# Second products of experts and MLP: activations held in the array, 512 weight features passing

## The chip, the cores and the metric

The kernel runs on one core of one Trainium2 chip. The metric is the device time of one execution in microseconds; the kernel before took 3621.57 us (median of three runs, 3618.63 to 3621.67). TensorE multiplies, VectorE (DVE), ScalarE (ACT) and GpSimd (POOL) do the elementwise work, and SyncE (SP) issues the loads.

## The reference, cut to what matters

256 tokens of 2048 features pass through two blocks. The first ends with a layer of 16,384 experts, of which each token takes 128 with gates; the second ends with an MLP of 8192 hidden features. What the change touches are the last lines of the two:

```python
    # experts (block 1): rows of exp_v, summed with the weights of the chosen experts
    a = jax.nn.gelu(jnp.einsum('cd,chkd->chk', xc, u))
    w = gc * a
    out = jnp.einsum('chk,chkd->cd', w, exp_v[ec])
    ...
    # MLP (block 2)
    x = x + jnp.square(jax.nn.relu(h2 @ w_up[l])) @ w_down[l]
return rmsnorm_2(x, g_final)
```

## The kernel before, in words

All activations lie with features on the 128 partitions and the 256 tokens in the columns. Nothing is gathered: every expert is multiplied for every token, and the gate of an expert that was not chosen is zero. So the experts are two dense products with 16,384 hidden features, in 16 groups of 1024 (8 tiles of 128), and the MLP is the same with 8 groups of 1024.

Every product runs in three parts. `load_half` (L163) loads 128 x 1024 fp32 weights into `raw` (4 buffers), ScalarE rounds them into `wh` (L168), and VectorE takes the rest into `wl` (L169); `wh` and `wl` have 3 buffers each. Activations are a `Pair` of a rounded part and a rest. `mm3` (L186) then gives high times high (L187), high times rest (L188) and rest times high (L189). The first operand of `T.matmul` stands in the array (its load is the LDWEIGHTS, in the profile PEld), the second passes.

The second product of a group is `down` (L1233). It runs over 16 tiles of 128 output features; `gemm_tile` (L206) sums 8 hidden tiles into 256 columns of a bank `mm`, 24 matmuls of 128 weight features in the array and 256 tokens passing. So a group has 16 x 24 = 384 matmuls and takes 16 halves of weights. After each tile a function is called. For the experts it is `moe_done` (L1276): group 0 copies the bank into `total` on ScalarE, groups 1 to 14 add it there on VectorE (L1282), group 15 adds it, times `g2`, to the stream `xs` (L1286), sums the squares of the stream for two norms (`ss3`, `ss4`: a Square on ScalarE (L273) into one of two buffers `sqt`, then an addition (L274), on POOL for the first 14 tiles), and makes the first operand `hp` of block 2 (L286, L287). For the MLP it is `mlp_done` (L1541), which adds each bank to the stream (L1543) and in the last group sums its squares.

A scheduler sets the order of each engine's instructions from the order in which the program is written and its own costs; each engine then takes them strictly in that order. `total` uses two buffers `act`. After group 15 come the two sums over partitions (L224), the turned norms (L253) and, among them, the first products of block 2 (`w_in2`, from L1373 on). Banks: `mm` has 3, `aux` 3 and `acc` 2 buffers of [128, 512] fp32.

Of the kernel before, what the change touches and what calls it, by code (L numbers as in the profile page):

```python
# [17 lines left out]
L = 256  # L18
# [9 lines left out]
# groups of experts whose first products go ahead  # L28
AHEAD = 7
# blocks of 512 modulation values that TensorE takes, and tiles of 128 that VectorE takes  # L30
PE_ADA = [4, 5, 6, 7, 0, 1, 2, 3, 8, 9, 10, 11]
DVE_ADA = list(range(48, 96))
# buffers of raw weights, of their parts, of the modulation's tiles, and of gates that wait for branches
NRAW, NW, NADR, NGT = 4, 3, 2, 18
# the gates of 4 tokens: microseconds of VectorE, and how many steps their rows go ahead of their products
GATE_COST, LEAD = 1.8, 2
# tiles of the modulation for VectorE after each weight tile of a phase of block 1
SLOW = ([1] * 9, [0] * 4, [0] * 6 + [1] * 2, [2] * 4, [1] * 16)
# microseconds of VectorE for the work that waits, after each weight tile
PEER_PUMP, MIX_PUMP = (2.6, 2.6, 3.5), (1.8, 1.8, 2.0, 1.8)  # L40

# columns of the packed per-channel vectors
# [12 lines left out]
# columns of the constants, which depend on shapes alone  # L55
# [8 lines left out]
# those that stay, those of the state space operators, those of the attention  # L64
# [10 lines left out]
def body(top, tc, nc, V, S, G, T, I, out):  # L75
# [28 lines left out]
    # ---------------------------------------------------------------- constants  # L104
# [19 lines left out]
    # work that fills in between weight tiles: (cost on VectorE in us, function)  # L124
# [24 lines left out]
    # ------------------------------------------------- weights: load and split  # L149
# [5 lines left out]
    def load_behind(dst, src):  # L155
        """A load that waits for its turn behind the weights before it."""
        if last_load[0] is None:
            nc.sync.dma_start(dst, src)
        else:
            with tc.issue_after(ins_of(last_load[0])):  # L160
                nc.sync.dma_start(dst, src)
# [13 lines left out]
    # where the modulation's tiles go, and how many  # L175
# [15 lines left out]
    class Pair:  # L191
        """Activations as float32r high and low parts, 8 feature tiles to a buffer."""
# [8 lines left out]
    def split(dst, src, eng=None):  # L201
        """dst = (high, low) of the fp32 src."""
        S.activation(dst[0], src, AF.Copy)
        V.tensor_tensor(dst[1], src, dst[0].bitcast(F32), op=OP.subtract)
# [8 lines left out]
    # ------------------------------------------------------------------- norms  # L213
    def row_sum(acc):
        """Sum of acc over partitions, on every partition."""
# [4 lines left out]
    def token_sum(acc):  # L220
        """Sum of acc over partitions, by tokens on partitions [128, 2]."""
# [8 lines left out]
    def rsqrt_tok(m):  # L230
        """1/sqrt(m); a Newton step after the engine's square root."""
# [9 lines left out]
    def rstd_tok(p, n):  # L241
        """1/sqrt(p/n + eps) of sums by tokens."""
# [4 lines left out]
    def spread_tok(y, turned=False):  # L247
        """A value by token, from [128, 2] to every partition [128, L]; turned: from tokens (j, c) to (c, j)."""
# [28 lines left out]
    def scaled_pair(dst, src, gain, rstd, shift, scp):  # L277
        """dst pair = src * gain * rstd + shift."""
# [5 lines left out]
    def gained(dst, src, gain):  # L284
        """dst pair = src * gain."""
# [3 lines left out]
    # ================================================================== block 1  # L289
# [9 lines left out]
    # silu(c), by partitions in column 0 of a block of 32 for TensorE, and on every partition for VectorE  # L299
# [11 lines left out]
    def early_raw():  # L311
        """Before the products start, buffers of later uses take the tiles too: one or two pieces."""
# [7 lines left out]
    def ada_parts(b, early=False):  # L320
        """512 modulation values: four column groups of the array take four row tiles at a time."""
# [42 lines left out]
    # the norm of the input  # L364
# [5 lines left out]
    # products of the state space inputs run block by block of features: two tiles in a bank, opened with zeros  # L370
# [5 lines left out]
    # columns: sh1, sc1, g1, sh2, sc2, g2  # L376
# [4 lines left out]
    def u_block(b):  # L381
        """What 512 features give to the state space inputs."""
# [23 lines left out]
    # ---- SSM parameters, on [(parity, state), pair of groups]  # L406
# [91 lines left out]
    def cmul(ore, oim, are, aim, bre, bim, t1, t2, minus=None, eng=V):  # L498
        """o = a * b; with minus = -are, the imaginary part with its sign turned."""
# [7 lines left out]
    def ssm_params():  # L507
        dt = expo(ld)
        # exp and sin, cos of the exponent of a and of its multiples that the tables start from
# [11 lines left out]
        # powers a^0 .. a^4 and the input weights a^(3-j) * w  # L521
# [29 lines left out]
        # phasor tables: e^(i 4 theta b) and e^(i 32 theta a)  # L551
# [17 lines left out]
        # the input weights, by [j, part, pair] rows, to DRAM  # L569
# [16 lines left out]
    def ssm_pre(t):  # L586
        """The operators of four pairs of groups: of the inputs, of the states, and within a chunk."""
# [43 lines left out]
    # ---------------------------------------------------------------- SSM tiles  # L631
# [6 lines left out]
    def ssm_store_u(t, p):  # L638
        """Channels (parity, h, pair) and tokens 4c + j, to rows (parity, j, h) and columns (pair, c)."""
# [8 lines left out]
    def ssm_in(t):  # L648
# [4 lines left out]
        # taps by distance, then by input and output place in the chunk  # L653
# [15 lines left out]
        # chunk inputs, turned back by the phase at the chunk  # L669
# [74 lines left out]
    # feature tiles 0-1 k_cmp, 2-3 v_cmp, 4 gates, 5-6 k_slc, 7-8 k_win, 9-16 q, 17-20 v  # L744
# [33 lines left out]
    # ------------------------------------------------------- compressed keys  # L778
# [7 lines left out]
    def compress(s):  # L786
        """Keys (s = 0) by features, values (s = 1) by key rows: four column groups of the array, 32 blocks in each."""
# [47 lines left out]
    # gates to token rows  # L835
# [440 lines left out]
    def moe_done(d, p):  # L1276
        xt, sm = xs[d // 8][:, d % 8], total[d // 8][:, d % 8]
        if g == 0:
            S.activation(sm, p, AF.Copy)  # L1279
            return  # L1280
# [425 lines left out]
```

## Time and profile before

| what | value |
|---|---|
| median of three runs | 3621.57 us |
| profiled execution, span | 3613.3 us |
| matmuls of the second products of the experts | 3 x 2048 |
| matmuls of the second products of the MLP | 3 x 1024 |
| last expert group ends | 2193 us |
| last matmul of the MLP starts | 3596.02 us |

The profiled execution's own time is not listed apart from its span; the median stands 8.3 us over the span. In the page, a matmul's mean time includes the time that it needs from its first column to its end, and neighbours overlap in it: the pace of a stretch is read from the distance of starts or from the count in a stretch, not from the mean.

### The profile page before, as it was taken

Reading aid. Unit: us, or ns where it says so; the run is one execution under the profiler, and the core shown is the slowest. Engines: PE = TensorE matmul, PEld = TensorE weight load, DVE = VectorE, ACT = ScalarE, POOL = GpSimd, SP = SyncE. Lnnn points to the kernel's source line nnn. Section 1 sums busy time; section 2 is a strip of 40 time slices with the busy share of each in tenths; the row PEclk is TensorE's granted clock in tenths of the full one; section 3 lists DMA queues with packets and bytes.
Section 4 is the critical chain, followed back from the end, with each engine's and each line's share of the span. In section 5 each row is a group of like instructions: output and inputs, shape, how many; then the busy total and the mean of one; then the engine's idle time right before and its main releaser. Section 6 shows DMA issues by size and latency. Waiting matters only on the chain.

```text
span 3613.3 us, 71254 instructions
## 1 busy us (share of the span) xinstructions
PE 3525.4 (98%) x29284; PEld 3421.0 (95%) x29284; DVE 2485.9 (69%) x4064; ACT 1667.9 (46%) x2438; POOL 355.2 (10%) x318
## 2 busy tenths in 40 slices
PE   6899988999999999999999999999999999999998
PEld 3678888999999999999999999999999999999998
DVE  6485888899967555555555679887655666666665
ACT  2234844469954444444444445345444443343444
POOL 3442041016600000000000012000000000000000
PEclk8899999999999999999999999999999999999999
DMA  8888685556677666666656655555555555555554
GB/s 312 313 293 287 237 312 176 176 180 223 234 247 239 220 217 218 220 216 219 196 193 208 218 183 179 186 176 180 184 184 182 181 182 185 182 184 184 182 184 143
DMA packets 227749, 759.76 MB, mean 210 GB/s; under 512 B 26888, under 2 KB 64144, under 8 KB 211936
## 3 DMA queue, kind: packets, MB, share of 16 engines
q1 hardware_dynamic: 219440, 747.27, 61.1%
q0 software_dynamic: 1648, 5.57, 0.5%
q8 instruction: 230, 3.77, 0.4%
q10 hardware_dynamic: 6336, 2.36, 0.2%
q14 instruction: 95, 0.78, 0.1%
HBM read 731.91 MB, written 23.21 MB: 209 GB/s over the span
## 4 chain that ended last, share of the span: by engine, by line
PE 88%; DVE 6%; DMA 2%; issue 1%; ACT 1%; POOL 1%; ACTq 0%; SPq 0%; DVEq 0%; POOLq 0%
PE mm L189 27%; PE mm L187 27%; PE mm L188 27%; DVE wl L169 2%; PE acc L333 1%; DVE gst L1206 1%; POOL t L1030 1%; DVE oh L1187 1%; ACT wh L168 1%; DVE oh L1186 0%; DVE va L1361 0%; PE u L403 0%; PE aux L340 0%; PE aux L658 0%; DMA udr<-t 0%
## 5 line engine op out<-in xcount | busy, mean ns | idle before, releaser
L168 ACT ACTIVATE wh<-raw 128x1024 fp32r<-128x1024 f32 x1126 | 1190.0, 1059 | 1654.1 <-PE mm L188 1465.4
L169 DVE TENSOR_TENSOR wl<-raw,wh 128x1024 fp32r<-128x1024 f32 x1126 | 1382.9, 1231 | 640.3 <-ACT wh L168 628.7
L189 PE MATMUL mm<-hp,wl 128*128 128x256 f32 x5168 | 1470.6, 285 | 4.9 <-DVE wl L169 4.9
L187 PE MATMUL mm<-hp,wh 128*128 128x256 f32 x5168 | 1470.0, 285 | 4.3 <-ACT hp L281 2.5
L188 PE MATMUL mm<-hp,wh 128*128 128x256 f32 x5168 | 1467.0, 284 | 0.8 <-DVE hp L282 0.8
L187 PEld LDWEIGHTS mm<-hp,wh 128*128 128x128 f32 x5168 | 993.9, 193 | 12.0 <-issue 5.2
L189 PEld LDWEIGHTS mm<-hp,wl 128*128 128x128 f32 x5168 | 994.2, 192 | 10.6 <-DVE wl L169 7.3
L188 PEld LDWEIGHTS mm<-hp,wh 128*128 128x128 f32 x5168 | 994.4, 193 | 5.7 <-issue 4.1
L187 PE MATMUL mm<-p,wh 128*128 128x256 f32 x2048 | 579.9, 283 | 0.9 <-ACT act L1279 0.9
L188 PE MATMUL mm<-p,wh 128*128 128x256 f32 x2048 | 579.7, 283 | 0.0
L189 PE MATMUL mm<-p,wl 128*128 128x256 f32 x2048 | 579.5, 283 | 0.0
L187 PEld LDWEIGHTS mm<-p,wh 128*128 128x128 f32 x2048 | 393.5, 192 | 1.1 <-ACT act L1279 1.1
L188 PEld LDWEIGHTS mm<-p,wh 128*128 128x128 f32 x2048 | 393.5, 192 | 0.0
L189 PEld LDWEIGHTS mm<-p,wl 128*128 128x128 f32 x2048 | 393.2, 192 | 0.2 <-DVE wl L169 0.2
L187 PE MATMUL mm<-hid,wh 128*128 128x256 f32 x1024 | 289.8, 283 | 0.0
L188 PE MATMUL mm<-hid,wh 128*128 128x256 f32 x1024 | 289.8, 283 | 0.0
L189 PE MATMUL mm<-hid,wl 128*128 128x256 f32 x1024 | 289.8, 283 | 0.0
L187 PEld LDWEIGHTS mm<-hid,wh 128*128 128x128 f32 x1024 | 196.6, 192 | 0.0
L188 PEld LDWEIGHTS mm<-hid,wh 128*128 128x128 f32 x1024 | 196.6, 192 | 0.0
L189 PEld LDWEIGHTS mm<-hid,wl 128*128 128x128 f32 x1024 | 196.6, 192 | 0.0
L1282 DVE TENSOR_TENSOR act<-mm,act 128x256 f32<-128x256 f32 x224 | 95.0, 424 | 123.1 <-PE mm L189 123.1
L1190 POOL TENSOR_TENSOR row<-oh,gl 128x512 fp32r<-128x512 f32 x64 | 137.1, 2158 | 304.1 <-DVE gl L1264 222.7
(448 smaller groups left out, 3549.3 us busy)
## 6 DMA issues: line engine op xcount, KB each, us to landing
raw<-in_peer_u SPq DMA_DIRECT2D x256, 512.0 KB, 4.2
raw<-in_peer_v SPq DMA_DIRECT2D x256, 512.0 KB, 4.2
raw<-in_w_up SPq DMA_DIRECT2D x128, 512.0 KB, 3.6
raw<-in_w_down SPq DMA_DIRECT2D x128, 512.0 KB, 3.7
raw<-in_w_in SPq DMA_DIRECT2D x110, 512.0 KB, 4.4
adr<-in_w_ada_dve SPq DMA_DIRECT2D x48, 1024.0 KB, 6.6
raw<-in_w_gate SPq DMA_DIRECT2D x96, 512.0 KB, 3.5
adr<-in_w_ada_pe SPq DMA_DIRECT2D x32, 1024.0 KB, 5.6
```

What stands on the lines that cost most here:

```text
L168: S.activation(wh, r, AF.Copy)
L169: last_split[0] = ins_of(V.tensor_tensor(wl, r, wh.bitcast(F32), op=OP.subtract))
L187: T.matmul(p, w[0], x[0], start=st, stop=False)
L188: T.matmul(p, w[0], x[1], start=False, stop=False)
L189: T.matmul(p, w[1], x[0], start=False, stop=sp)
L333: T.matmul(p[32 * j:32 * j + 32], csel[:, 4 * c + j], raws[j // n][:, 512 * (j % n):512 * (j % n) + 512], start=(c == 0), stop=(c == 3), t ...
L1030: G.tensor_tensor(t1, t1, t2, op=OP.add)
L1187: V.tensor_tensor(oh2, io, fan(eslot[:, 1]), op=OP.is_equal)
L1190: G.tensor_tensor(row[:, :, 1], oh1, fan(gl), op=OP.mult)
L1206: V.tensor_tensor(o, p[:, :, 1], o, op=OP.add)
L1282: V.tensor_tensor(sm, p, sm, op=OP.add)
```

## The change

`down` is turned round. What stands in the array is now a 128-token half of an activation part, and 512 weight features pass. For each of 4 blocks `c` of 512 output features it takes two banks (one for each half of the tokens, `acc` for even and `aux` for odd blocks) and sums all 8 hidden tiles into them: 4 halves of weights, each with 2 hidden tiles and 12 matmuls of 512 columns. A group so has 4 x 48 = 192 matmuls instead of 384, and as many columns pass in all. The sums lie by token rows: `total` and, for the MLP, a new `summed` are added to from the two banks, 512 columns at a time (in the changed file L1251 for the first group, L1253 for the others). Only in the last group of each (`d_done` given) the four feature tiles of a block are turned back by 8 transposes (L1260) into `mm` banks and the old function is called on them. The stream is added to once, and not in each MLP group. The weights' layout on the host changes to match (`_tm`).

```diff
-    def down(src, w, d_done):
-        for dp in range(8):
-            hv = load_w(src[dp])
-            for f in range(2):
-                p = gemm_tile(hv, list(range(8 * f, 8 * f + 8)), w)
-                d_done(2 * dp + f, p)
+    def down(src, w, total, first, d_done=None):
+        for c in range(4):
+            ps = [aux_bank() if c % 2 else acc_bank() for _ in range(2)]
+            for q in range(4):
+                wh, wl = load_half(src[c, q])
+                for e in range(2):
+                    xh, xl = w[2 * q + e]
+                    cols = slice(512 * e, 512 * e + 512)
+                    for i, p in enumerate(ps):
+                        t = slice(128 * i, 128 * i + 128)
+                        T.matmul(p, xh[:, t], wh[:, cols], start=(q + e == 0), stop=False)
+                        T.matmul(p, xl[:, t], wh[:, cols], start=False, stop=False)
+                    for i, p in enumerate(ps):
+                        T.matmul(p, xh[:, 128 * i:128 * i + 128], wl[:, cols], start=False, stop=(q == 3 and e == 1))
+            for i, p in enumerate(ps):
+                o = total[i].rearrange("p a t -> p (a t)")[:, 512 * c:512 * c + 512]
+                if first:
+                    S.activation(o, p, AF.Copy)
+                else:
+                    V.tensor_tensor(o, p, o, op=OP.add)
+            if d_done is None:
+                continue
+            for d in range(4 * c, 4 * c + 4):
+                p = mm_bank()[:, :L]
+                for i in range(2):
+                    T.transpose(p[:, 128 * i:128 * i + 128],
+                                total[i].rearrange("p a t -> p (a t)")[:, 128 * d:128 * d + 128], ident)
+                d_done(d, p)
...
     def moe_done(d, p):
-        xt, sm = xs[d // 8][:, d % 8], total[d // 8][:, d % 8]
-        if g == 0:
-            S.activation(sm, p, AF.Copy)
-            return
-        if g < NG - 1:
-            V.tensor_tensor(sm, p, sm, op=OP.add)
...
+        xt = xs[d // 8][:, d % 8]
         V.scalar_tensor_tensor(xt, p, g2[:, d:d + 1], xt, op0=OP.mult, op1=OP.add)
...
-        down(I["peer_v"][g], w, moe_done)
+        down(I["peer_v"][g], w, total, g == 0, moe_done if g == NG - 1 else None)
...
+    summed = [tl(ml, [128, 8, L], F32, "sum", 2) for _ in range(2)]
...
-        down(I["w_down"][g], hid.pop(g), mlp_done)
+        down(I["w_down"][g], hid.pop(g), summed, g == 0, mlp_done if g == 7 else None)
```

Three places show how the instructions move. The first is TensorE inside the last expert group (`p` are the weighted activations, rounded part and rest); before:

```order
L187 MATMUL mm_25855<-p_3719_25235,wh_25817 128x256
L188 MATMUL mm_25855<-p_3720_25236,wh_25817 128x256
L189 MATMUL mm_25855<-p_3719_25235,wl_25818 128x256
L187 MATMUL mm_25855<-p_3719_25235,wh_25817 128x256
L188 MATMUL mm_25855<-p_3720_25236,wh_25817 128x256
L189 MATMUL mm_25855<-p_3719_25235,wl_25818 128x256
```

and after:

```order
L1244 MATMUL acc_22117<-wh_22121,p_3599_22099 128x512
L1245 MATMUL acc_22117<-wh_22121,p_3600_22100 128x512
L1244 MATMUL acc_22118<-wh_22121,p_3599_22099 128x512
L1245 MATMUL acc_22118<-wh_22121,p_3600_22100 128x512
L1247 MATMUL acc_22117<-wl_22122,p_3599_22099 128x512
L1247 MATMUL acc_22118<-wl_22122,p_3599_22099 128x512
```

Two hidden tiles gave six matmuls of 256 columns for one tile of 128 features; one hidden tile now gives six of 512 columns for four such tiles.

The second place is TensorE where the last expert group ends and block 2 begins (`hp` is the operand of block 2, `mm_25958` its first sum). Before:

```order
L188 MATMUL mm_25855<-p_3720_25236,wh_25817 128x256
L189 MATMUL mm_25855<-p_3719_25235,wl_25818 128x256
L187 MATMUL mm_25958<-hp_25249,wh_25948 128x256
L188 MATMUL mm_25958<-hp_25251,wh_25948 128x256
L189 MATMUL mm_25958<-hp_25249,wl_25949 128x256
```

After (`mm_22678` is that sum):

```order
L1247 MATMUL aux_22485<-wl_22544,p_3599_22099 128x512
L1247 MATMUL aux_22486<-wl_22544,p_3599_22099 128x512
L1260 MATMUL mm_22561<-con_71,act_1170_6339 128x128
L1260 MATMUL mm_22573<-con_71,act_1170_6339 128x128
L1260 MATMUL mm_22585<-con_71,act_1170_6339 128x128
L1260 MATMUL mm_22561<-con_71,act_1171_6340 128x128
L1260 MATMUL mm_22573<-con_71,act_1171_6340 128x128
L1260 MATMUL mm_22585<-con_71,act_1171_6340 128x128
L1260 MATMUL mm_22597<-con_71,act_1170_6339 128x128
L1260 MATMUL mm_22597<-con_71,act_1171_6340 128x128
L187 MATMUL mm_22678<-hp_22113,wh_22668 128x256
```

The eight transposes of the last block stand directly behind its last matmul and ahead of block 2. Those of each of the three blocks before stand in three pieces inside the next block, the first behind its first 3 or 4 matmuls, the last behind 9 or 10.

The third place is ScalarE in the last expert group, where it rounds weights (L168) between the work for the feature tiles (L273 Squares, L286 operand of block 2). Before:

```order
L286 ACTIVATE hp_25249<-b_950_5035,gmix_12531 128x256
L168 ACTIVATE wh_25491<-raw_25489 128x1024
L273 ACTIVATE sqt_25401<-b_950_5035 128x256
L273 ACTIVATE sqt_25404<-b_950_5035,vec_73 128x256
L286 ACTIVATE hp_25249<-b_950_5035,gmix_12531 128x256
L168 ACTIVATE wh_25497<-raw_25495 128x1024
```

After (`wh_22295` is the last quarter of the second block):

```order
L273 ACTIVATE sqt_22217<-b_950_5035 128x256
L273 ACTIVATE sqt_22220<-b_950_5035,vec_73 128x256
L286 ACTIVATE hp_22113<-b_950_5035,gmix_12531 128x256
L273 ACTIVATE sqt_22229<-b_950_5035 128x256
L273 ACTIVATE sqt_22232<-b_950_5035,vec_73 128x256
L286 ACTIVATE hp_22113<-b_950_5035,gmix_12531 128x256
L168 ACTIVATE wh_22295<-raw_22293 128x1024
L168 ACTIVATE wh_22365<-raw_22363 128x1024
L168 ACTIVATE wh_22383<-raw_22381 128x1024
```

One tile's three instructions alternated with one rounding of weights; now the twelve of four tiles stand in a row, and the roundings behind them in a row.

## Rows read from the trace of the kernel before

**Rows 1.** Page, part 1: busy us (share of the span) xinstructions.

```profile
PE 3525.4 (98%) x29284; PEld 3421.0 (95%) x29284; DVE 2485.9 (69%) x4064; ACT 1667.9 (46%) x2438; POOL 355.2 (10%) x318
```

**Rows 2.** Waits of TensorE, 1040 to 3600 us, the longest: us, times, longest us.

```profile
PE aux L224 <- DVE ssq L274: 1.4, 1, 1.4
```

**Rows 3.** Page, part 5, second products: xcount | busy us, mean ns | idle before.

```profile
L187 PE MATMUL mm<-p,wh 128*128 128x256 f32 x2048 | 579.9, 283 | 0.9 <-ACT act L1279 0.9
...
L187 PE MATMUL mm<-hid,wh 128*128 128x256 f32 x1024 | 289.8, 283 | 0.0
```

**Rows 4.** Stretches: PE, PEld, DVE, ACT, POOL busy (instructions), PEclk, DMA, GB/s.

```profile
1037.00:1039.90 2.90, 2.90 (x16) 2.90 (x15) 2.89 (x5) 1.45 (x2) 0.00 (x0) 0.50 0.92 302
1200.00:1400.00 200.00, 200.00 (x1669) 200.00 (x1668) 115.85 (x125) 82.66 (x97) 0.00 (x0) 1.00 0.66 222
...
3200.00:3400.00 200.00, 200.00 (x1669) 200.00 (x1668) 121.00 (x157) 79.69 (x88) 0.00 (x0) 1.00 0.56 184
```

**Rows 5.** Timeline of TensorE in the experts: start us, us, engine line.

```profile
2000.05 0.28 PE L187 MATMUL mm<-p,wh 128*128 128x256 f32 x1
2000.17 0.28 PE L188 MATMUL mm<-p,wh 128*128 128x256 f32 x1
```

**Rows 6.** Timeline of the weight loads at the same place.

```profile
2000.05 0.19 PEld L188 LDWEIGHTS mm<-p,wh 128*128 128x128 f32 x1
```

**Rows 7.** Timeline of TensorE in the stretch of granted clock 0.50.

```profile
1038.36 0.41 PE L187 MATMUL mm<-hp,wh 128*128 128x256 f32 x1
1038.58 0.41 PE L188 MATMUL mm<-hp,wh 128*128 128x256 f32 x1
```

**Rows 8.** Timeline of TensorE, two starts twelve matmuls apart, behind a wait.

```profile
516.72 0.28 PE L189 MATMUL mm<-qy,wl 128*128 128x256 f32 x1
...
518.11 0.28 PE L189 MATMUL mm<-hp,wl 128*128 128x256 f32 x1
```

**Rows 9.** Timeline of TensorE, three merged runs: one-column products, slower products, transposes.

```profile
232.74 1.02 PE L340 MATMUL aux<-ones,adaz 128*128 128x1 f32 x8
...
370.30 1.03 PE L818 MATMUL aux<-con,cz 128*128 128x256 f32 x4
...
410.61 0.82 PE L943 MATMUL aux<-con,lg 128*128 128x128 f32 x6
```

**Rows 10.** Groups of ScalarE and VectorE; the last: ns shortest, median, longest.

```profile
L168 ACT ACTIVATE wh<-raw 128x1024 fp32r<-128x1024 f32 x882 | 933.6, 1059 | 1413.0 <-PE mm L188 1292.1 <-issue 89.3 <-DVE co L1402 9.1
...
L169 DVE TENSOR_TENSOR wl<-raw,wh 128x1024 fp32r<-128x1024 f32 x883 | 1079.7, 1225 | 543.7 <-ACT wh L168 532.3
...
L1226 DVE TENSOR_TENSOR act<-act,p x40: 682/686/695, 1029.7 to 2066.6; 128x512 f32<-128x512 f32 x40
```

**Rows 11.** Timeline of POOL, VectorE and ScalarE for the squares and the stream.

```profile
558.68 0.74 POOL L274 TENSOR_TENSOR ssq<-ssq,sqt 128x256 f32<-128x256 f32 x1 [1.11 <-ACT sqt L273]
...
2157.14 2.35 POOL L274 TENSOR_TENSOR ssq<-ssq,sqt 128x256 f32<-128x256 f32 x2 [0.53 <-ACT sqt L273]
...
2158.82 0.47 DVE L1286 SCALAR_TENSOR_TENSOR b<-mm,g,b 128x256 f32<-128x256 f32 x1
...
2160.20 0.49 ACT L286 ACTIVATE hp<-b,gmix 128x256 fp32r<-128x256 f32 x1
```

**Rows 12.** Timeline of TensorE where the experts end.

```profile
2192.89 0.28 PE L189 MATMUL mm<-p,wl 128*128 128x256 f32 x1
2193.01 0.28 PE L187 MATMUL mm<-hp,wh 128*128 128x256 f32 x1
...
2200.86 0.64 PE L253 MATMUL aux<-diag,ones 128*128 128x256 f32 x2
```

**Rows 13.** Timeline where the MLP ends.

```profile
3596.02 0.28 PE L189 MATMUL mm<-hid,wl 128*128 128x256 f32 x1
...
3597.25 0.42 DVE L274 TENSOR_TENSOR ssq<-ssq,sqt 128x256 f32<-128x256 f32 x1 [0.48 <-ACT sqt L273]
```

More of the change, by code (lines that the diff above doesn't have):

```diff
@@ L1276, in moe_done @@
     def moe_done(d, p):
-        xt, sm = xs[d // 8][:, d % 8], total[d // 8][:, d % 8]
-        if g == 0:
-            S.activation(sm, p, AF.Copy)
-            return
-        if g < NG - 1:
-            V.tensor_tensor(sm, p, sm, op=OP.add)
-            if g == NG - 2:
-                V.scalar_tensor_tensor(xt, sm, g2[:, d:d + 1], xt, op0=OP.mult, op1=OP.add)
-            return
+        xt = xs[d // 8][:, d % 8]
         V.scalar_tensor_tensor(xt, p, g2[:, d:d + 1], xt, op0=OP.mult, op1=OP.add)
@@ L1539, in body, with mlp_done @@
             mlp_up(g + 1)
-        def mlp_done(d, p, last=(g == 7)):
+        def mlp_done(d, p):
             xt = xs[d // 8][:, d % 8]
             V.tensor_tensor(xt, p, xt, op=OP.add)
-            if last:
-                ss6.add(xt)
-                S.activation(xt, xt, AF.Copy, scale=VC("g_final")[:, d:d + 1])
-        down(I["w_down"][g], hid.pop(g), mlp_done)
+            ss6.add(xt)
+            S.activation(xt, xt, AF.Copy, scale=VC("g_final")[:, d:d + 1])
+        down(I["w_down"][g], hid.pop(g), summed, g == 0, mlp_done if g == 7 else None)
     r6 = rstd_of(ss6.acc, D)
@@ L1562, in _fm, with _tm @@
     return np.ascontiguousarray(w.reshape(k // 128, 128, f // 128, 128).transpose(2, 1, 0, 3)).reshape(f // 128, 128, k)
+def _tm(w):
+    return w.reshape(-1, 4, 2, 128, 4, 512).transpose(0, 4, 1, 3, 2, 5).reshape(-1, 4, 4, 128, 1024)
 def _cols(v):
@@ L1621, in layout @@
     r["peer_u"] = a["peer_u"][0].reshape(128, 128, 16, 128).transpose(0, 3, 2, 1).reshape(128, 128, D)
-    r["peer_v"] = a["peer_v"][0].reshape(128 // GE, GE, 128, 8, 2, 128).transpose(0, 3, 2, 4, 1, 5).reshape(128 // GE, 8, 128, D)
+    r["peer_v"] = _tm(a["peer_v"][0])
     w = a["w_in_2"][0].reshape(D, 34, 128)
@@ L1632, in layout @@
     r["w_up"] = _fm(a["w_up_2"][0])
-    r["w_down"] = a["w_down_2"][0].reshape(8, 8, 128, 8, 2, 128).transpose(0, 3, 2, 4, 1, 5).reshape(8, 8, 128, D)
+    r["w_down"] = _tm(a["w_down_2"][0])
     dsk = a["ssm_d"][0].reshape(32, 2, 16).transpose(1, 2, 0)
```

## The prediction

> **What bounds the kernel now.** I read the page first: TensorE is busy 98% of the span [rows 1]. Busy time of overlapping matmuls is no pace, so I went on to the waits. From 1040 us to the end of the MLP TensorE has five waits in the list, the longest 1.4 us in total [rows 2]. So in that part the time is matmuls times pace, and a count divided into a stretch gives the pace: 1669 matmuls in 200 us of experts, and again 1669 in 200 us of MLP, are 119.8 ns each at granted clock 1.00, which is the 2.4 GHz level [rows 4]. The timeline shows the same, starts 0.12 us apart [rows 5]. The mean of 283 ns [rows 3] is no pace, since neighbours overlap.
>
> 256 columns at 2.4 GHz, one a cycle, would be 106.7 ns. What are the other 13 ns? Three views help. In a stretch at granted clock 0.50 (1.2 GHz) starts are 0.21 to 0.22 us apart [rows 7], and 256 / 1.2 = 213.3: where the columns pass slowly, nothing is added. Eight matmuls of a single column, each with its own load of 128 columns, take 1.02 us, the last 0.27 of it its own length: (1.02 - 0.27) / 7 = 107 ns, so loads alone have a pace near that of 256 columns [rows 9]. And each load starts together with the matmul before its own [rows 5, 6]. My reading: the next load takes up to 120 ns from there, and a matmul whose columns pass in 107 ns waits for it. With 512 columns (213.3 ns) the load is over long before.
>
> The four products at L818 pass 256 columns slowly at the full clock: (1.03 - 0.38) / 3 = 217 ns [rows 9], about 213.3 and 2 to 4 more. So I take 215.7 ns for the new matmul: 213.3 and the 2.4 ns between that row's reading (up to 217) and the bare stream. Bounds: 213.3 (nothing added) and 240 (120 ns per 256 columns, whatever the cause).
>
> The Trainium skill, "TensorE: Matmul & The Clock Gate", section "Back-to-back issue gap", gives the isolated gap as 262 cycles for 256 columns and 518 for 512, that is 109 and 216 ns. The second is my value; the first is contradicted by 119.8 ns here. By the page alone the change would save 9216 x 109 - 4608 x 216 = 9 us, less than it costs; the measurement decides for the old matmul, and no run here shows the new one.
>
> **The change part by part.**
>
> *Matmuls.* Removed: 3 x 2048 and 3 x 1024 [rows 3], 9216 x 120 ns = 1105.9 us. Added: 24 groups x 192 = 4608 x 215.7 = 993.9 us. Gain 112.0 us; by the bounds 123 (at 213.3) and 0 (at 240).
>
> *Weights.* A half of weights serves 12 matmuls, 2.59 us instead of 24 x 0.12 = 2.88. Rounding and rest take 1.06 + 1.23 = 2.29 us one after the other, on two engines [rows 10], so neither is over half busy with it, and three buffers put two halves (5.2 us) between a split and its use. DMA must bring 512 KB in 2.59 us, 202 GB/s; 302 stand in the rows at one place, 222 in the experts [rows 4]. Taken as nothing; without that cover it is the rival below.
>
> *Sums.* 16 additions of 256 columns become 8 of 512, 0.69 us each by the addition of that size [rows 10], while TensorE works on the other pair of banks for 10.4 us. Nothing on the path.
>
> *Transposes.* 64. Six in a row take 0.82 us, so (0.82 - 0.27) / 5 = 0.11 each [rows 9]: 7.0 us of TensorE, 3.5 in each last group. The Trainium skill, same page, section "Part 4: PE-mode transpose", puts one at about 275 ns inside a kernel; by that it would be 17.6 us and the time some 10 us more. The run of six decides for 0.11.
>
> *Last expert group.* Here I expect the largest loss. The feature tiles now come four at once, every 10.4 us. Each needs two Squares on ScalarE, which write two buffers that POOL empties by additions. POOL takes 2.35 us for two additions beside VectorE's work and 0.74 for one alone [rows 11]. With VectorE less busy in the burst I take 0.93 each, nearer to the lone one. ScalarE takes its twelve instructions for four tiles in order, and the rounding of the block's last quarter of weights stands behind them. From the end of the block before: two sums (2 x 0.62), a transpose (0.3) and the stream's update (0.47 [rows 11]) bring the first Square to 2.4 us; its addition starts at 2.8. The eighth Square waits for the sixth addition, 2.8 + 6 x 0.93 = 8.4; Square and operand, 0.4 + 0.49 [rows 11], end at 9.3, then 1.06 + 1.23 of splitting: 11.6. TensorE wants that quarter after three quarters and the transposes, 3 x 2.59 + 0.9 = 8.7. So a block waits some 3 us; the first has two additions fewer and waits 1.4. In the third that rounding is ahead of the burst, but then block 2's first weights are behind it, and the last sums stand behind those on VectorE. Following the four queues row by row with these durations, blocks two to four take 2.9, 4.0 and 1.4 us over 10.35 (transposes in it), 6.9 us pass between the last matmul and block 2's first, where it was 0.12 [rows 12], and 1.6 us more are lost to the norms' sums (before, the norm's product came 7.85 us behind block 2's first matmul [rows 12]). Together 16.8. With additions of 0.74 it is 13, with 1.18 it is 22. Take 17.
>
> *Last MLP group.* Here VectorE adds the squares, and no POOL. Mid-group transposes 24 x 0.11 = 2.6 us and three short waits for the sums, 0.3 each. At the end, the square's addition of the last tile ended 3597.67 - 3596.02 = 1.65 us behind the last matmul's start [rows 13]; now two sums (to 1.5), transposes (to 1.8) and four tiles with updates, Squares and scalings in turn on ScalarE, 0.9 each, end at about 5.3. Plus 3.7; nothing hides it, as everything behind it is serial. Together 7, bounds 5 and 11. Saved additions to the stream in groups 1 to 7 were hidden and give nothing.
>
> Sum: 112 - 17 - 7 = 88 us off 3613.3, 3525.3; with the 8.3 us that the median stands over that span, **3533.6 us**. Its own range: pace 213.3 to 218 (gain 123 to 101), costs 18 to 33, and up to 10 more of short waits: 3517 to 3564.
>
> **The rivals.**
>
> *The extra 13 ns stays with every matmul* (a fixed price of a change of weights): 226.6 ns, gain 4608 x 13.4 = 62 instead of 112: 3584 us. For it: 119.8 is steady. Against it: at half clock nothing is added [rows 7]. 6%.
>
> *Weights come late.* Between two expert groups VectorE multiplies and splits the weighted activations, 8 operations of 0.69 us = 5.5 us [rows 10]. If they stand in one piece, a rest is late by 5.5 - (2 x 2.59 - 2.29) = 2.6 us; 16 groups, 42 us: 3576. Against it: cover was only 0.6 us larger before, and no such wait stands among the longest [rows 2]. 6%.
>
> *Slower: 120 ns is the pace at which 256 columns pass.* Then 512 take 240, the gain is nothing and the 24 us remain: 3646 us. It decides from 234.8 ns on (4608 x 5.2 = 24). For it: the constancy of 119.8, and half clock is too slow to show such a limit. Against it: behind a wait, twelve matmuls in a row start in 518.11 - 516.72 = 1.39 us, 116 ns each [rows 8], which a limit on the columns would not let pass. 8%. The page's table, by which 256 columns had nothing to lose, ends on this side too, 9 us gained for 24 paid: 3637. Its chance is in these 8%.
>
> **How the numbers follow.** Forecast 80%, rivals 6, 6 and 8%. The range: 3515 to 3570 holds the forecast's own range but for its rare ends, some three quarters, and the nearer part of the second rival. A measurement of this kernel tells 0.2% (7 us) from no change. Faster by more: the forecast and two rivals, less a little for costs that add up, 0.90; slower, the third rival, 0.08; within it, 0.02.
>
> **What would show it.** Starts of the 512-column matmuls 0.215 to 0.218 us apart (0.227 first rival, 0.24 third); 192 second products a group, near 192 x 0.2157 = 41.4 us where 384 x 0.12 = 46.1 were; in the last expert group TensorE waiting for the rounding of a block's last quarter, and about 7 us between its last matmul and block 2; at the end about 4 us more between the last matmul and the last addition of squares. I am wrong if the new pace is over 220, or if waits of TensorE on `wl` appear in the middle groups.

## The result and the profile after

The changed kernel takes 3582.36 us (median of four runs, 3578.11 to 3589.44) where the kernel before, run beside it, takes 3621.62: a ratio of 0.9899, 95% interval 0.9884 to 0.9915. So it is 1% faster, 39 us where 88 were forecast, and 12 us above the upper end of the range. The profiled execution took 3580.89 us, 1.8 over its span of 3579.1. One of the four executions of experiment 6 below took 5643 us, at a mean granted clock of 0.56, and is left out of its median.

First the page of the changed kernel, part 1, and one of its groups (columns as in [rows 1, 3]):

```profile
PE 3480.2 (97%) x24740; PEld 3190.7 (89%) x24740; DVE 2439.2 (68%) x3888; ACT 1671.5 (47%) x2438; POOL 340.5 (10%) x318
...
L1244 PE MATMUL acc<-wh,p 128*128 128x512 f32 x512 | 199.4, 389 | 0.8 <-ACT wh L168 0.8
```

TensorE is as full as before, and the new matmuls wait for nearly nothing. So what is missing should lie mostly in their pace. Stretches of the changed kernel inside the second products of one group and inside first products (start and end us, busy time of PE, PEld, DVE, ACT, POOL with instructions, granted clock, DMA):

```profile
1226.00:1266.00 40.00, 40.00 (x178) 33.13 (x177) 22.32 (x22) 15.88 (x17) 0.00 (x0) 1.00 0.61 200
1270.00:1310.00 40.00, 40.00 (x334) 39.87 (x334) 23.05 (x24) 18.58 (x25) 0.00 (x0) 1.00 0.68 223
```

The count takes in one or two matmuls that reach into a stretch, so starts are the sharper measure. Timeline of TensorE in the changed kernel (start us, length, line):

```profile
1950.24 0.39 PE L1244 MATMUL acc<-wh,p 128*128 128x512 f32 x1
1950.47 0.39 PE L1245 MATMUL acc<-wh,p 128*128 128x512 f32 x1
1950.69 0.39 PE L1244 MATMUL acc<-wh,p 128*128 128x512 f32 x1
```

Over the 192 matmuls of a middle group the starts lie 226.7 ns apart, not 215.7, in the experts and in the MLP. The old ones lie 120.0 apart [rows 5]. Both are the bare columns at 2.4 GHz and 13.3 ns: 213.3 + 13.3 and 106.7 + 13.3.

The time by stretches, in us, from the traces (the cut variant is the second experiment):

| stretch | before | changed | cut in 256 |
|---|---|---|---|
| first second product of the experts to the second of the four L253 behind the last | 1162.1 | 1134.9 | 1171.6 |
| from there to the first second product of the MLP | 749.9 | 748.9 | 748.9 |
| from there to the end of the span | 662.2 | 648.4 | 668.8 |

The three stretches give 27.2 + 1.0 + 13.8 = 42.0 us. The stretch ahead of them, which the change doesn't touch, is 7.9 us longer in this execution. The 1.0 belongs to the first stretch: in the changed kernel nine more matmuls of block 2, 1.1 us, stand ahead of that L253.

### The profile page after: what moved, and what is told of

Same layout as the page of the kernel before. It is cut to its first block, busy times and chain, and to the rows that moved or that the text cites. A ratio compares the mean times of both kernels' runs of the same rounds, so it can differ in the third digit from the quotient of the medians.

```text
span 3579.1 us, 61663 instructions
## 1 busy us (share of the span) xinstructions
PE 3480.2 (97%) x24740; PEld 3190.7 (89%) x24740; DVE 2439.2 (68%) x3888; ACT 1671.5 (47%) x2438; POOL 340.5 (10%) x318
## 5 line engine op out<-in xcount | busy, mean ns | idle before, releaser
L168 ACT ACTIVATE wh<-raw 128x1024 fp32r<-128x1024 f32 x1126 | 1190.1, 1059 | 1594.6 <-PE mm L188 841.3
L1244 PE MATMUL acc<-wh,p 128*128 128x512 f32 x512 | 199.4, 389 | 0.8 <-ACT wh L168 0.8
L1244 PE MATMUL aux<-wh,p 128*128 128x512 f32 x512 | 199.4, 389 | 0.0
L1245 PE MATMUL acc<-wh,p 128*128 128x512 f32 x512 | 199.3, 389 | 0.0
L1245 PE MATMUL aux<-wh,p 128*128 128x512 f32 x512 | 199.3, 389 | 0.0
L1247 PE MATMUL acc<-wl,p 128*128 128x512 f32 x512 | 158.5, 390 | 1.1 <-DVE wl L169 1.0
L1247 PE MATMUL aux<-wl,p 128*128 128x512 f32 x512 | 158.5, 390 | 0.1
L274 POOL TENSOR_TENSOR ssq<-ssq,sqt 128x256 f32<-128x256 f32 x40 | 36.1, 925 | 1156.5 <-ACT sqt L273 1156.5
L359 DVE SCALAR_TENSOR_TENSOR adr<-adr,b 128x2048 f32<-128x2048 f32 x48 | 111.3, 2319 | 31.8 <-DMA adr<-in_w_ada_dve 31.8
L1247 PEld LDWEIGHTS acc<-wl,p 128*128 128x128 f32 x512 | 95.9, 188 | 21.7 <-DVE wl L169 1.9
L1244 PEld LDWEIGHTS acc<-wh,p 128*128 128x128 f32 x512 | 96.2, 188 | 20.7 <-ACT wh L168 1.2
L1244 PEld LDWEIGHTS aux<-wh,p 128*128 128x128 f32 x512 | 96.1, 188 | 20.2 <-ACT wh L168 0.4
L1245 PEld LDWEIGHTS aux<-wh,p 128*128 128x128 f32 x512 | 96.1, 188 | 19.9
```

What stands on the lines that cost most here:

```text
L168: S.activation(wh, r, AF.Copy)
L274: eng.tensor_tensor(self.acc, self.acc, t, op=OP.add)
L359: V.scalar_tensor_tensor(raw, raw, 1.0, cb, op0=OP.mult, op1=OP.mult, accum_out=ada[:, j:j + 1])
L1244: T.matmul(p, xh[:, t], wh[:, cols], start=(q + e == 0), stop=False)
L1245: T.matmul(p, xl[:, t], wh[:, cols], start=False, stop=False)
L1247: T.matmul(p, xh[:, 128 * i:128 * i + 128], wl[:, cols], start=False, stop=(q == 3 and e == 1))
```

## Experiments

The theory after the first look is A: 13.3 ns come with every matmul of these kernels, whatever its columns. That is the first rival of the prediction. What it hangs on was open: the change of the operand in the array, the sum, the bank, the data, the rows or columns in use, or the type.

**1. Lone runs.** Nothing of the computation is left; TensorE runs series with one thing changed in each, such as

```diff
+    for i in range(n):   # new form
+        T.matmul(p[i % 2], x[:, w(i)], r[:, m(i)], start=i < 2, stop=i > n - 3)
+    for i in range(n):   # one operand all along
+        T.matmul(p[i % 2], x[:, 0:128], r[:, m(i)], start=i < 2, stop=i > n - 3)
+    for i in range(n):   # bf16
+        T.matmul(p[i % 2], b[:, w(i)], b[:, m(i)], start=i < 2, stop=i > n - 3)
```

> This kernel leaves out the whole computation. TensorE alone runs 480 matmuls in the form of the new second products (rounded fp32, 128x128 in the array, 512 columns passing, banks in turn, accumulating), then runs of 96 in which one thing is changed. The changed kernel shows 226.7 ns where I had forecast 215.7; the old form 120.0. Theory A, a fixed price of each matmul, whatever its columns: 384 columns take 160 + 13.3 = 173.3 ns, 256 take 120, and no other single change moves 226.7. Rivals: B, the price of changing the operand in the array: with one and the same 128x128 all along 213 and 107 ns. C, of accumulating or of changing the bank: with every matmul a new sum, or all in one bank, 213. D, of the data (switching): with zeros 213. E, of the 4-byte operands: with bf16 213 to 216 for 512 and 107 to 109 for 256 columns. F, of the rows or columns of the array: 64 rows, or 64 columns, 213. The plain fp32 form of 256 columns shows 213 to 217 per record in the kernels, nothing or up to 4 ns added.

Groups of TensorE in this kernel (operation, shapes, count, busy us in all, mean ns of one). A series of 96 has 95 distances, so the pace is (busy - mean) / 95:

```profile
L116 PE MATMUL p<-r,x 128*64 128x512 f32 x96 | 22.3, 393 | 0.0
L124 PE MATMUL p<-r,x 128*128 128x512 f32 x96 | 22.1, 391 | 0.0
L114 PE MATMUL p<-r,x 64*128 64x512 f32 x96 | 22.1, 388 | 0.0
L108 PE MATMUL p<-r,x 128*128 128x512 f32 x96 | 22.0, 390 | 0.0
L100 PE MATMUL p<-r,x 128*128 128x512 f32 x96 | 21.9, 389 | 0.0
L110 PE MATMUL p<-r,x 128*128 128x512 f32 x96 | 21.9, 389 | 0.0
L112 PE MATMUL p<-z 128*128 128x512 f32 x96 | 21.9, 389 | 0.0
L118 PE MATMUL p<-b 128*128 128x512 bf16 x96 | 20.9, 379 | 0.0
L122 PE MATMUL p<-raw 128*128 128x256 f32 x96 | 20.9, 379 | 0.0
L106 PE MATMUL p<-r,x 128*128 128x384 f32 x96 | 16.8, 334 | 0.0
L104 PE MATMUL p<-r,x 128*128 128x256 f32 x96 | 11.7, 283 | 0.0
...
L120 PE MATMUL p<-b 128*128 128x256 bf16 x96 | 10.6, 273 | 0.0
```

The new form itself (L124, run last) takes (22.1 - 0.39) / 95 = 228 ns. One operand all along (L100), one bank (L110), zeros (L112): (21.9 - 0.39) / 95 = 226 ns each. A new sum with every matmul (L108) 227, half the rows (L114) 228, half the columns of the array (L116) 231. 384 columns (L106) take 173, 256 (L104) 120. So rivals C, D and F fall, and A holds as far as columns go. But bf16 takes (20.9 - 0.38) / 95 = 216 ns for 512 columns and 109 for 256, as rival E said: **the 11 ns on top go with the rounded fp32 type.** Plain fp32 (L122, 48 instructions, two records each) shows 216 ns a record. A record of 256 columns is as long as 512 columns of bf16: it was this row's kind [rows 9] that I had taken for the price of 512 columns.

Rival B is not settled by this. The loads of the array in the same kernel:

```profile
L122 PEld LDWEIGHTS p<-raw 128*128 128x128 f32 x96 | 18.2, 190 | 2.4
...
L100 PEld LDWEIGHTS p<-r,x 128*128 128x128 f32 x96 | 18.0, 188 | 3.7
...
L116 PEld LDWEIGHTS p<-r,x 128*64 128x64 f32 x96 | 12.8, 134 | 9.4 <-issue 0.4
...
L118 PEld LDWEIGHTS <-b 128*128 128x128 bf16 x96 | 9.3, 98 | 11.4 <-issue 0.3
```

With one operand all along (L100) the array is still loaded 96 times, so this series never took the load away, and a price of 13.3 ns for each load would look the same as one for each matmul. The length of the load is not the price: loads of half the columns last 134 ns instead of 188 (L116) and the pace is no better, and plain fp32, with loads of 190 ns (L122), adds only 2.5 ns to a record. Why the type costs this, in its load or in its matmul, stays open.

The Trainium skill, "TensorE: Matmul & The Clock Gate", section "Back-to-back issue gap", gives 262 and 518 cycles, 109 and 216 ns. The bf16 series agree to the nanosecond; rounded fp32 lies 11 above both.

**2. The cut variant: 512 columns in two of 256.** Orientation, sums and transposes stay. All three products are cut in this way, as here the second:

```diff
...
-                        T.matmul(p, xl[:, t], wh[:, cols], start=False, stop=False)
+                        for o, cols in parts:
+                            T.matmul(p[:, o], xl[:, t], wh[:, cols], start=False, stop=False)
...
```

> The changed kernel with each matmul of 512 weight features cut into two of 256, one after the other, with the same activations in the array. Orientation, sums, transposes and loads stay. Theory A (13.3 ns with each matmul): 9216 matmuls at 120.0 instead of 4608 at 226.7, so 4608 x 13.3 = 61 us more than the changed kernel, about 3642. Rival B (the price belongs to the change of the operand in the array, and every second matmul keeps its operand): 226.7 for a pair, the time of the changed kernel, 3581.

3634.59 us, ratio to before 1.0038 (1.0026 to 1.0049): 14 us slower than the kernel before, some 52 slower than the changed one by the medians. A stretch of it inside a second product:

```profile
1230.00:1270.00 40.00, 40.00 (x336) 40.00 (x335) 21.27 (x21) 15.36 (x16) 0.00 (x0) 1.00 0.57 191
```

The pace is the old 120 ns, although every second matmul keeps its operand. Here too the array is loaded for each (335 loads to 336 matmuls), so a price of the load is not told from one of the matmul. But the whole gain of the change is the number of matmuls, each with its load. And since the count is now that of before, this kernel shows what turning back costs by itself: 9.5 us in the experts and 6.6 in the MLP, less 1.0 between (table).

By the table it is 36.7 + 20.4 = 57.1 us slower than the changed kernel, where 61 were expected. The experts lack 4.3 us of their part. Between the last second product and block 2 this kernel loses 3.6 us where the changed one loses 5.8, and behind its pause the granted clock is 1.00, where it falls in the changed kernel (experiment 9).

**3. and 4. Cross products as bf16.** If the price belongs to the type, two of three products can be rid of it: high times rest and rest times high carry only a correction, and bf16 is enough for a correction of this size. This makes the arithmetic a little coarser. The rests are written as bf16, and of a high part the upper halves are read.

```diff
+    def top(a):
+        return a.bitcast(BF16)[:, 1::2]
...
-                        T.matmul(p, xl[:, t], wh[:, cols], start=False, stop=False)
+                        T.matmul(p, xl[:, t], top(wh[:, cols]), start=False, stop=False)
...
-                        T.matmul(p, xh[:, 128 * i:128 * i + 128], wl[:, cols], start=False, stop=(q == 3 and e == 1))
+                        T.matmul(p, top(xh[:, 128 * i:128 * i + 128]), wl[:, cols], start=False, stop=(q == 3 and e == 1))
```

> The changed kernel; in the second products of experts and MLP the two cross products (rest of the activations times high weights, high activations times rest of the weights) pass as bf16: VectorE writes the rests as bf16, and of the high parts TensorE reads the upper two bytes of each element (every second 16-bit element), so no instruction is added. High times high stays in rounded fp32. Theory E (the extra 11 to 13 ns belongs to the rounded fp32 type, as the lone runs show with 215.9 ns for bf16): 3072 matmuls at 216 instead of 226.7, 33 us less than the changed kernel, about 3548. Rival: elements two bytes wide with a step of four bytes are read slower, or the change of type between neighbours costs: no gain, 3581 or more.

> As the run before, and the cross products of the experts' first products and of all of block 2 as bf16 too, there both operands by their upper halves; block 1 up to the choice of experts stays in rounded fp32. Theory E: 3072 + 2 x (2048 + 2848) = 12864 matmuls 10.8 ns shorter, 139 us less than the changed kernel, about 3443, if splitting the weights (2.3 us per half on two engines) still keeps up with a half used up in 2.7 us instead of 2.9. Rival (weights late, or strided reads slow): well above 3500.

Both failed: 3593.14 us (ratio 0.9926, 0.9908 to 0.9944) and 3592.71 (0.9927, 0.9907 to 0.9947), some 10 us slower than the changed kernel instead of 33 and 139 faster. In the first, a second product ran like this:

```profile
1240.04 0.58 PE L1251 MATMUL aux<-wh,p 128*128 128x512 f32 x1
1240.46 0.40 PE L1252 MATMUL aux<-wh,p 128*128 128x512 bf16 x1
1240.50 0.59 PE L1251 MATMUL aux<-wh,p 128*128 128x512 f32 x1
1240.93 0.40 PE L1252 MATMUL aux<-wh,p 128*128 128x512 bf16 x1
1241.17 0.59 PE L1254 MATMUL aux<-wl,p 128*128 128x512 bf16 x2
1241.41 0.58 PE L1251 MATMUL aux<-wh,p 128*128 128x512 f32 x1
```

From L1251 at 1240.04 to the same place of the next six at 1241.41 are 1.37 us, 229 ns each. The starts are uneven: 0.42 us from an fp32 matmul to a bf16 one, 0.04 back.

**5. Lone runs of these forms** tell a step in the operand from a change of type.

> The whole computation is left out. After the same 480 matmuls, runs of 96 with the operands read as upper halves: both strided with 512 and 256 columns, one strided and one plain bf16 either way, then the series high, cross, cross as in the two kernels with 512 and with 256 columns. Theory E: 216 and 109 ns wherever both operands are bf16; the series (226.7 + 2 x 216) / 3 = 219.5 and (120 + 2 x 109) / 3 = 113 on average. Rival: strided operands no faster than 226.7 and 120.

Groups of TensorE, then a piece of the timeline, of the second lone kernel:

```profile
L109 PE MATMUL p<-r,b 128*128 128x512 bf16 x96 | 21.8, 387 | 0.0
L103 PE MATMUL p<-r,x 128*128 128x512 bf16 x96 | 21.8, 386 | 0.0
L107 PE MATMUL p<-b,x 128*128 128x512 bf16 x96 | 20.9, 379 | 0.0
...
L105 PE MATMUL p<-r,x 128*128 128x256 bf16 x96 | 11.0, 274 | 0.0
```

```profile
200.39 0.58 PE L111 MATMUL p<-r,x 128*128 128x512 f32 x1
200.81 0.40 PE L112 MATMUL p<-r,b 128*128 128x512 bf16 x1
201.05 0.38 PE L113 MATMUL p<-b,x 128*128 128x512 bf16 x1
201.08 0.58 PE L111 MATMUL p<-r,x 128*128 128x512 f32 x1
```

A step of four bytes in the operand in the array (L107) costs nothing: (20.9 - 0.38) / 95 = 216. In the passing operand (L109, L103) it costs nearly what the type did: 225, and with 256 columns (L105) 113. And series of fp32, bf16, bf16 take 201.08 - 200.39 = 0.69 us (687 ns over the whole series) where the three alone make 227 + 225 + 216 = 668 ns: some 19 ns for a change of type and back, with 256 columns 360 instead of 120 + 113 + 113 = 346. These figures account for experiments 3 and 4. Six matmuls of 3 with two changes and back make 2 x (227 + 225 + 216 + 19) = 1374 ns, and 1.37 us were measured. Three products of 256 columns at 360 ns gain nothing against 3 x 120, so 4 ends where 3 does.

**6. to 8. In series, without a step, and in the old orientation.** In 6 (of the changed kernel) every half of weights of a first product gives first its high products, then its cross products:

```diff
...
+                for b, k in part:
+                    T.matmul(p, block(halves, b)[0], x[k][0], start=b == blocks[0], stop=False)
+                for b, k in part:
...
+                    T.matmul(p, top(wh), xl, start=False, stop=False)
+                    T.matmul(p, top(wl), xb, start=False, stop=b == blocks[-1])
...
```

In its second products only rest times high activations passes as bf16, behind the eight others of a half; those stay in rounded fp32. In 7 block 2's activations, but not the MLP's hidden ones, have a bf16 rest and a bf16 copy of the high part (`S.activation(dst[2], src, AF.Copy)`). Experiment 8 starts from the kernel before: old `down`, no transposes. There both cross products pass as bf16 in series in the second products too.

> The changed kernel with bf16 cross products as in the last kernel but set in series: for each half of weights first all high times high (rounded fp32), then all 16 cross products of the half as bf16; in the second products high and rest times high weights stay rounded fp32, and only the 4 products of a half with the rest of the weights follow as bf16. Theory: each change from one type to the other and back costs 13 ns with 256 columns and 18 with 512 (the series of three in the lone runs: 359 instead of 346, 687 instead of 669), a passing operand with a step of four bytes 113 instead of 109, and 120 remains for high times high. 306 tiles x (32 x 7 - 2 x 13) = 61 us and 384 halves x (4 x 10.7 - 18) = 10 us: 71 us less than the changed kernel, about 3511. Rival: in the kernel, neighbours' traffic or the split of weights holds TensorE whatever the type: within 15 us of 3581.

> As the run before, and in block 2 the rests of the activations are written as plain bf16, with a bf16 copy of the high part beside them (one more ScalarE operation for each activation tile, no more memory), so that the passing operand of the cross products has no step: 109 instead of 113. Theory: 178 tiles x 32 x 3.8 ns = 22 us less than the run before, about 3489. Rival: the step of the passing operand costs nothing in the kernel: the same time.

> The kernel before (weights in the array, 256 tokens passing in the second products) with the cross products of all of these products in series as bf16: 8 high times high, then 16 cross products. First products as in the run before: 128 x 198 + 178 x 320 ns = 82 us. Second products: 384 tiles x (16 x 10.8 - 13 to 26) = 56 to 61 us. About 3620 - 140 = 3480. If the 13 ns of the rounded fp32 type are all that the change saves, this kernel is within 15 us of the run before, on either side, as it has none of the costs of turning back (20 us in the traces). Rival: the change's orientation has a worth of its own, and this kernel is over 25 us slower than the run before.

| | time, us | ratio to before (95%) | expected |
|---|---|---|---|
| 6, changed kernel, in series | 3527.34 | 0.9734 (0.9715 to 0.9754) | 3511 |
| 7, and no step in block 2 | 3505.39 | 0.9680 (0.9663 to 0.9696) | 3489 |
| 8, the kernel before, in series, no step | 3483.92 | 0.9615 (0.9599 to 0.9631) | 3480 |

Stretches of first and second products in 6, of a first product of the MLP in 7, and of first and second products of the experts in 8, in this order:

```profile
1260.00:1300.00 40.00, 40.00 (x347) 35.75 (x347) 23.52 (x25) 18.70 (x25) 0.00 (x0) 1.00 0.69 226
```

```profile
1217.00:1257.00 40.00, 40.00 (x178) 26.51 (x177) 23.60 (x24) 16.95 (x17) 0.00 (x0) 1.00 0.65 216
```

```profile
2914.00:2954.00 40.00, 40.00 (x358) 36.79 (x356) 26.32 (x36) 17.96 (x23) 0.00 (x0) 1.00 0.57 193
```

```profile
1262.00:1302.00 40.00, 40.00 (x347) 35.71 (x347) 23.48 (x25) 19.75 (x27) 0.00 (x0) 1.00 0.70 233
1306.00:1346.00 40.00, 40.00 (x356) 36.84 (x356) 25.58 (x32) 16.07 (x16) 0.00 (x0) 1.00 0.63 219
```

Over whole tiles of the traces, a type change and back included, first products of the experts take 116.1 ns a matmul, of the MLP in 7 113.3, old second products in 8 113.1. Counted from these, 306 x 48 x 3.9 = 57 us for 6 (measured against the changed kernel: 55); 128 x 48 x 3.9 + 178 x 48 x 6.7 = 81 for 7 (77); with 9216 x 6.9 = 64 more 145 for 8 (measured against the kernel before: 138). Part of what lacks in 8 are waits for rests of weights, 6.4 us where the kernel before has 0.8:

```profile
PE mm L234 <- DVE wl L171: 6.4, 6, 1.9
```

The step from 6 to 7 came out as expected, 22 us. My estimate of 6 was 16 us too good. A tile saved 187 ns instead of 198. And the second products, with four bf16 matmuls in twelve, gained nothing where I had counted 10 us: a half of weights takes 2727 ns, 227 a matmul. The fp32 matmuls between the bf16 ones start 224 to 236 ns apart. Why stays open.

Kernel 8 is the fastest, 21 us faster than 7. That fits neither side of its expectation, within 15 us or over 25 slower. Nor does it test the orientation alone: in 7 two of three second products are rounded fp32, in 8 one of three. A half of weights takes 2727 ns of second products in 6 and 24 x 113.1 = 2714 in 8, so the 21 us are about what turning back costs (20). A turned kernel with both cross products as bf16 in series was not run. That the orientation has nothing left to give is therefore not shown; that the old one reaches more than the turn by getting rid of rounded fp32 is.

**9. Work put into the pause.** In the changed kernel, the end of the experts looks like this (timeline of TensorE, in brackets the wait and who ended it):

```profile
2164.43 0.61 PE L1247 MATMUL aux<-wl,p 128*128 128x512 f32 x2
2167.91 1.28 PE L1260 MATMUL mm<-con,act 128*128 128x128 f32 x6 [2.87 <-DVE act L1253]
2170.17 0.69 PE L1260 MATMUL mm<-con,act 128*128 128x128 f32 x2 [0.97 <-DVE b L1302]
2170.65 0.55 PE L187 MATMUL mm<-hp,wh 128*128 128x256 f32 x1
...
2172.07 0.41 PE L187 MATMUL mm<-hp,wh 128*128 128x256 f32 x1
2172.28 0.41 PE L188 MATMUL mm<-hp,wh 128*128 128x256 f32 x1
```

Behind the pause starts are 0.21 us apart. The stretch shows why, granted clock 0.50, that is 1.2 GHz:

```profile
2168.80:2175.60 6.80, 5.83 (x28) 5.28 (x27) 6.05 (x14) 4.79 (x12) 2.99 (x4) 0.50 0.59 214
```

The experiment puts 36 matmuls of block 2, whose operands are there, ahead of the transposes:

```diff
+    def ahead():
+        first["w"] = load_w(I["w_in2"][0])
+        first["p"] = mm_bank()[:, :L]
+        for k in range(12):
+            mm3(first["p"], block(first["w"], k), last[k], k == 0, False)
```

> The changed kernel; in the last expert group the first tile of block 2 (its features 0 to 11 of 16, 36 matmuls, 4.3 us) is written ahead of the last block's transposes, its last 12 matmuls behind them. In the changed kernel 5.8 us pass there between the end of the last second product and block 2, and the granted clock is 0.50 for 6.8 us from near the end of the pause, which lengthens some 24 matmuls from 120 to 213 ns, 2.2 us. Theory: the pause shrinks to the wait for the sums and the operands of the last four tiles, under 3 us in pieces, the clock stays at 1.00, and block 2's first products end 4 to 7 us earlier against the last second product. Rival: the chain of the last four tiles (sums, transposes, operands) ends last anyway, so the time is lost in front of the 12 matmuls instead: less than 2 us earlier.

The longest waits of TensorE in it around this place, and its 60 us behind the last second product under those of the changed kernel:

```profile
PE mm L189 <- DVE wl L169: 1.4, 2, 0.8
PE mm L1262 <- DVE b L1304: 0.8, 1, 0.8
```

```profile
2164.70:2224.70 60.00, 55.30 (x430) 53.80 (x429) 53.90 (x108) 29.50 (x41) 2.99 (x4) 0.94 0.49 158
```

```profile
2168.65:2228.65 60.00, 57.20 (x457) 55.03 (x456) 55.89 (x112) 30.40 (x43) 2.98 (x4) 1.00 0.49 165
```

The clock stays at 1.00, the longest wait shrinks from 2.9 to 0.8 us, and in 60 us 27 matmuls more are done, 27 x 0.12 = 3.2 us. That lies between theory and rival: the waits listed in these 60 us only fall from 4.7 to 2.9 us. In the time of the whole, 3581.97 us (0.9890, 0.9874 to 0.9907), 3 us can't be seen.

## Why the prediction was wrong, step by step

- **Matmuls: the step that failed.** I read 13 ns as a wait for a load that outlasts 106.7 ns, which 512 columns would hide, and so took 215.7. Measured: 226.7, so 4608 x 13.3 = 61 us instead of 112. The wait is not there: the same 13.3 ns stand on 256, 384 and 512 columns, though the columns of 384 pass in 160 ns and those of 512 in 213. The supports were of the wrong kind. The slower products and the one-column products of [rows 9] are plain fp32, another type; a record of 256 columns lasts like 512 of bf16, and the one-column row is of eight records, two to an instruction. And [rows 7] show nothing added at half clock; that says nothing about the full clock, as 512 columns last as long at the full clock as 256 at half, and there 13.3 ns are added.
- **The first rival came nearest**, with 3584 us against 3582 measured. I gave it 6%, and the range ended 14 us below it. Its support, a steady 119.8 in every stretch, was direct evidence on this form; what spoke against it came from other forms. Its 13 ns with every matmul are borne out; its cause, a change of weights, is not shown (experiment 1). And [rows 8], 116 ns a matmul behind a wait, stay unexplained: in such places starts lie 113 to 120 ns apart for some tens of matmuls before the steady 120. That the total is within 2 us is partly luck, as its costs (24 us) and its 8.3 us outside the span are both off.
- **Weights and sums** cost nothing, as forecast: between 1046 and 2110 us TensorE has one wait for weights in the list, 1.0 us.

```profile
PE acc L1247 <- DVE wl L169: 1.0, 1, 1.0
```

- **Transposes**: starts in a run mostly 0.11 us apart, as forecast. But the matmul behind a run comes late too: the eight of a block in the middle of a group lengthen it by 1.0 us, 0.13 each. The length of one has a median of 273 ns, near the 275 of the Trainium skill, "TensorE: Matmul & The Clock Gate", section "Part 4: PE-mode transpose": that figure is a length, and the prediction's 17.6 us used it as a pace.
- **Last expert group: 12.8 us, 17 forecast.** That is 16 x 192 x 13.33 ns less the 28.2 of the table (27.2 and the 1.0 that belongs to it). POOL's additions took 0.742 us (median), about the lower of the bounds, for which 13 stood there. The last group loses 5.2 us in its blocks, 3.0 of it transposes, instead of 8.3; only the rounding ahead of one block was late, by 0.8. The pause is 5.8 us, 6.9 forecast. The 1.6 us for the norms' sums are not there: no wait for them stands in the list behind the pause. The additions of 512 columns, put at 0.69 us in one place of the prediction and at 0.62 in another, take 0.68. Not foreseen: the 2.2 us at half clock. So the sum came near partly because misses cancel.
- **Last MLP group: 6.6 us (8 x 192 x 13.33 ns less 13.8), 7 forecast.** Its blocks lose 3.1 us, all of it transposes; the three short waits for the sums are not there. Where the MLP ends in the changed kernel, to be held against [rows 13]:

```profile
3558.19 0.61 PE L1247 MATMUL aux<-wl,hid 128*128 128x512 f32 x2
3558.62 1.29 DVE L1253 TENSOR_TENSOR sum<-aux,sum 128x512 f32<-128x512 f32 x2 [4.88 <-PE aux L1247]
3559.36 1.14 PE L1260 MATMUL mm<-con,sum 128*128 128x128 f32 x6 [0.56 <-DVE sum L1253]
...
3562.67 0.95 DVE L274 TENSOR_TENSOR ssq<-ssq,sqt 128x256 f32<-128x256 f32 x2 [0.25 <-ACT sqt L273]
```

  The last addition of squares ends at 3563.62, 5.2 us behind the last matmul's start at 3558.42; 1.65 before, 5.3 forecast.
- **Outside the span** I added 8.3 us, the median of before less its span. The profiled execution of the changed kernel has 1.8. In that execution the untouched first stretch was 7.9 us longer, so the two nearly cancel.

The sum as it should have been: 61.4 - 12.8 - 6.6 = 42.0 us. The two costs in it are what the table leaves; read one by one, 5.2 + 5.8 + 2.2 in the experts and 3.1 + 3.6 at the end of the MLP give about the same. The path was right and the costs were near, 24 us forecast and 19 measured. The gain was mis-sized, at 112 us for 61, because the reading of the 13 ns behind it was wrong.

## What to carry to other kernels

Before a pace is taken for a new shape, split the old pace into columns and a rest, and price the rest by a row of the same type: a rest that is the same in every stretch is better carried over than explained away. Fewer, longer matmuls save that rest once per matmul and no more, so look whether a type without it does the job: here cross products as bf16, in series of one type and with no step in the passing operand, gave 138 us in the old orientation, over three times what the turn gave. And what a turn leaves behind is paid at the ends of a stage, where a pause of some us can cost clock too.

## What the runs showed of the hardware

- Rounded fp32 at granted clock 1.00 (2.4 GHz): columns and 13.3 ns (120, 173, 227 for 256, 384, 512); bf16 about 2.5 ns (109, 216 for 256, 512). Plain fp32: two records of 216 ns for 256 columns.
- A series with one operand all along loads the array for every matmul all the same (96 loads for 96 matmuls).
- A step of four bytes in the passing bf16 operand: 225 and 113 ns instead of 216 and 109; in the operand in the array none.
- A change of type and back: 19 ns in a series of three with 512 columns, 14 with 256.
- Behind a pause of 5.8 us, of which TensorE worked 1.9, the granted clock was 0.50 for 6.8 us; with the same place filled it stayed at 1.00, and so it did in the cut variant behind a pause of 3.6 us, of which TensorE worked 1.8.
